# FFN weight sums in another order: A11 and A12 split as one tile, S3 and S2 made first, and the last product of a pair ahead of the next pair's S4

## The chip, the cores and the metric

The kernel runs on one core of one Trainium2 chip. The time is device microseconds of one execution. The kernel before takes 1554.56 us in the median of 3 runs (1554.34 to 1556.42).

## The reference

Two layers of a diffusion transformer work on 256 latent tokens and 256 context tokens, D = 1024, in float32. Layer 0 mixes the tokens by a short convolution, layer 1 by grouped-query attention. Around each mixer stand two gated FFNs, each of them modulated by shift, scale and gate of a conditioning vector:

```
def _swiglu(h, w13, w2):
    gte, up = jnp.split(h @ w13, 2, axis=-1)
    return (jax.nn.silu(gte) * up) @ w2
...
lat = lat + 0.5 * mod[:, 0, 2] * _swiglu(_modulate(lat, norm_g[i, 0], mod[:, 0, 0], mod[:, 0, 1]), ffn_w13[i, 0], ffn_w2[i, 0])
```

w13 is 1024 x 5632 and w2 is 2816 x 1024. In three of the four FFNs, (layer, block) = (0,0), (0,1) and (1,0), latent and context tokens go through the same weights, so that the kernel works on 512 columns of tokens; in the last, (1,1), only the 256 latent tokens are left. The change bears on the w13 product of the first three.

## The kernel before, in words

**Layout and precision.** Activations are held transposed, features on the 128 partitions and tokens along the free axis. Each float32 product is made of three matmuls on two parts of each operand (`mm3`, L133): hi x hi, hi x lo, lo x hi. The weights are split on the chip (`split`, L107): ScalarE (ACT) copies the raw tile to hi (L108), VectorE (DVE) subtracts hi from raw to make lo (L109). Raw tiles have eight buffers (`wr`, 1024 wide), hi and lo four each (`wh`, `wl`, 1024 wide, from `half`). `split_far` (L113 to L115) makes a lo without DVE: ACT writes hi and then -hi, and a DMA of GpSimd's queue adds the weight from memory onto it. Its tiles `w4h` and `w4l` have two buffers each.

**An FFN.** The hidden features come in 22 tiles of 128, cut into thirds of 8, 7 and 7 tiles (`THIRDS`). A third makes w13 for its tiles and then w2 (`project`, L581). In each FFN some first tiles are made in the plain way (six in (0,0), two in (0,1) and (1,0), by `w13_mm`, their results named pg and pu); all the others, 56 in the whole kernel, are *pairs*.

**A pair** (class `Pair`, L689 to L773) computes gate and up of one hidden tile by seven products in place of eight, in Winograd's form of Strassen's scheme. The weights of the tile are four blocks of 512 columns (up and gate, times the two halves of the features), A11, A12, A21 and A22, the activations four blocks of 256 tokens (B, with their sums T1 to T4). One product (`prod`) has four k-tiles of three matmuls, 128 x 256, into the banks p and q. The weight sums are S1 = A21 - A22 (as it is used here), S2 = A11 - S1, S3 = A22 - S2 and S4 = A12 - S2.

In `__init__` SyncE (SP) loads r2 (A22 and A12, 512 KB) and the right half of r1 (A11, 256 KB). GpSimd (POOL) writes the negation of r2's left half to r1's left half (L702), and a DMA of its queue adds A21 on it (L705): this is S1. A11 and A12 are split as two 512-wide pieces (L708 to L710). `sums(0)` makes S2 in r1's right half (L724), and `keep` splits r1 as S1 and S2. `sums(1)` copies A22 (`split_far` from r2's left half), subtracts S2 from both halves of r2 (L732) and splits r2 as S3 and S4.

**Order of the products.** `head` makes A11 and A12 (ACT copies p at L749), `five` S1 (copy L755), `six` S2 (copy L759) and S4, after which DVE adds q to the copy (L761) and ACT applies silu (L762); `seven` makes S3 and adds (L766), `four` makes A22, then gate times up (L772) and the split of the result into `gh` and `gl`. The loop in `ffn` delays `seven` and `four` into the next pair: A11, A12, S1, S3 of the previous pair, S2, S4, A22 of the previous pair. The last pair's `seven` and `four` are put between the first tiles of w2. After each pair `tick(0.9, at)` issues about one unit of modulation (DVE, L178), behind the previous pair's L766. The order on each engine and the semaphores come from a scheduling framework that follows the program's order and its dependences.

Of the kernel before, what the change touches and what calls it, by code (L numbers as in the profile page):

```python
# [16 lines left out]
P = 128  # L17
# [3 lines left out]
T2 = 2 * S  # L21
NM = 22
THIRDS = (8, 7, 7)

AS_IS = {(0, 0): range(3, 6), (0, 1): (), (1, 0): ()}

# [21 lines left out]
def hybrid_kernel(ctx: ExitStack, tc: tile.TileContext, a: dict, out: bass.AP):  # L48
# [640 lines left out]
    class Pair:  # L689
# [6 lines left out]
        def __init__(self, src, h):  # L696
            self.h, self.w, self.src = h, {}, src
            r2 = load_raw(src[:, 1024:2048])
            r1 = wp.tile([P, 1024], F32, name=nm("wr"), tag="wr", bufs=8)
            nc.sync.dma_start(r1[:, T2:], src[:, T2:1024])  # L700

            nc.gpsimd.tensor_scalar(  # L702
                out=r1[:, :T2], in0=r2[:, :T2], scalar1=-1.0, scalar2=None, op0=ALU.mult
            )
            nc.gpsimd.dma_start(out=r1[:, :T2], in_=src[:, :T2], accum_op=ALU.add)  # L705
            self.raw = [r1, r2]
            ts = half()
            for i, key in enumerate(("A11", "A12")):  # L708
                self.w[key] = [t[:, i * T2 : i * T2 + T2] for t in ts]
                split(*self.w[key], self.raw[i][:, T2:])  # L710

        def keep(self, keys, part):
            hi, lo = half()
# [4 lines left out]
        def sums(self, n):  # L718

            r1, r2 = self.raw  # L720
            s1, s2 = r1[:, :T2], r1[:, T2:]
            tt = nc.vector.tensor_tensor
            if n == 0:
                tt(out=s2, in0=s2, in1=s1, op=ALU.subtract)  # L724
                self.keep(("S1", "S2"), r1)
                return
            self.w["A22"] = [
                wp.tile([P, T2], F32R, name=nm(t), tag=t, bufs=2) for t in ("w4h", "w4l")
            ]
            split_far(*self.w["A22"], r2[:, :T2], self.src[:, 1024 : 1024 + T2])  # L730
            v = lambda t: t.rearrange("p (a c) -> p a c", a=2)
            tt(  # L732
                out=v(r2), in0=v(r2), in1=s2.unsqueeze(1).to_broadcast([P, 2, T2]),
                op=ALU.subtract,
            )
            self.keep(("S3", "S4"), r2)

        def prod(self, ps, wk, hk, first=True):
            for k in range(4):
# [14 lines left out]
            self.gm = tp.tile([P, T2], F32, name=nm("gm"), tag="gm", bufs=3)  # L754
            nc.scalar.copy(self.gm[:, S:], self.q1)  # L755

        def six(self):
            self.prod(self.p, "S2", "T2", False)
            nc.scalar.copy(self.sg[:, S:], self.p)  # L759
            self.prod(self.q1, "S4", ("B", 1, 1), False)  # L760
            nc.vector.tensor_tensor(out=self.sg, in0=self.q, in1=self.sg, op=ALU.add)  # L761
            nc.scalar.activation(out=self.sg, in_=self.sg, func=AF.Silu)  # L762
# [12 lines left out]
    def ffn(l, b, h, tot, gate, tail, gs=(), ev=(0, 0), z=None):  # L775
        gs = list(gs)
        i0 = 0
        for t, n in enumerate(THIRDS):
            between = ()
            if tot == T2:  # L780
                heads = []
                if t == 0 and not gs:

                    w = [load_w(a["w13"][l, b, 0])]
                    gs = [new_pair("g") for _ in range(2)]
                    pp = [(psum("pg"), psum("pu")) for _ in range(2)]
                    w13_mm(pp[0], w[0], h, range(KT), 0, S)
                    flush(1)
                    w.append(load_w(a["w13"][l, b, 1]))
                    at = w13_mm(pp[1], w[1], h, range(2), 0, S)  # L790
                    with tc.issue_after(at):
                        flush()
                    with tc.issue_after(every[-1]):
                        w13_mm(pp[1], w[1], h, range(2, KT), 0, S)
                    h.sums(0)
                    w13_mm(pp[0], w[0], h, range(KT), S, T2)
                    w13_post(pp[0], gs[0], 0, T2)
                    heads.append(Pair(a["w13"][l, b, 2], h))
                    h.sums(1)
                    heads[0].sums(0)  # L800
                    w13_mm(pp[1], w[1], h, range(KT), S, T2)
                    w13_post(pp[1], gs[1], 0, T2)
                    heads[0].head()
                    heads[0].sums(1)
                    h.sums(2)
                prev = None
                for i in range(len(gs), n):
                    if t == 0 and not heads and i in AS_IS[l, b]:
                        w = load_w(a["w13"][l, b, i])
                        pp = psum("pg"), psum("pu")  # L810
                        if prev:
                            prev.seven()
                        if "T1" not in h.t:
                            with tc.issue_after(rows["W1"]):
                                h.sums()
                        w13_mm(pp, w, h, range(4), 0, T2)
                        if prev:
                            gs.append(new_pair("g"))
                            prev.four(gs[-1])
                            prev = None  # L820
                        w13_mm(pp, w, h, range(4, KT), 0, T2)
                        gs.append(new_pair("g"))
                        tick(3, w13_post(pp, gs[-1], 0, T2))
                        continue
                    if heads:
                        pr = heads.pop(0)
                    else:
                        pr = Pair(a["w13"][l, b, i0 + i], h)
                        pr.sums(0)
                        pr.sums(1)  # L830
                        pr.head()
                    pr.five()
                    at = prev.seven().ins if prev else None
                    pr.six()
                    if prev:
                        gs.append(new_pair("g"))
                        prev.four(gs[-1])
                    prev = pr
                    if i:
                        tick(0.9, at)  # L840

                def last():
                    gs.append(new_pair("g"))
                    prev.four(gs[-1])

                between = (prev.seven, last) if prev else ()
            else:
                for i in range(n):
                    w = load_w(a["w13"][l, b, i0 + i])
                    gs.append(beside(gp.tile([P, T2], F32R, name=nm("gx"), tag="gh")))  # L850
                    pp = psum("pg"), psum("pu")
                    if i0 + i < EARLY:
                        for k in range(KT):
                            for j in range(2):
                                ps = pp[j][:, : z.w]
                                mm3(ps, w(at13(1 - j, k)), z.at(k), k == 0, k == KT - 1)
                            if i == 0 and k == KT // 2:
                                flush(1)
                        if i < 3:
                            flush(1)  # L860
                        early_post(pp, gs[i], z.ri)
                        tick(1)
                        continue
                    for j in range(2):
                        ws = [w(at13(1 - j, k)) for k in range(KT)]
                        mm_wide(pp[j], ws, [h.both(k) for k in range(KT)], True, True)
                    beside_post(pp, gs[i])
                    tick(1)
            i0 += n

            def ws2(m):
                src = a["w2a"][l, b, m // 2] if t == 0 else a["w2b"][l, b, t - 1, m // 2]
                o = (m % 2) * n * P
                raw = load_raw(src[:, o : o + n * P], n * P)
                hi, lo = half()
                split(hi[:, : n * P], lo[:, : n * P], raw[:, : n * P])
                return lambda k: (hi[:, k * P : k * P + P], lo[:, k * P : k * P + P])

            cur = gs
            end = t == len(THIRDS) - 1  # L880
            project(
                ws2,
                (lambda k, c0, c1: cur[k]) if tot == S
                else lambda k, c0, c1: (cur[k][0][:, c0:c1], cur[k][1][:, c0:c1]), n,
                gate, tail if end else None, tot, 2 if end and tot == T2 else 0, ev[end], between,
            )
            gs = []
# [527 lines left out]
def _layout(inp):  # L1415
# [17 lines left out]
    d["modb"] = f("mod_b").reshape(2, 72, P).transpose(2, 0, 1)  # L1433
    d["normg"] = f("norm_g").reshape(2, 3, KT, P).transpose(3, 0, 1, 2)
    w13 = f("ffn_w13").reshape(2, 2, 2, KT // 2, P, 2, NM, P)[:, :, :, :, :, ::-1]
    d["w13"] = w13.transpose(0, 1, 6, 4, 2, 5, 3, 7).reshape(2, 2, NM, P, 2048)
    w2 = f("ffn_w2").reshape(2, 2, NM, P, KT // 2, 2, P)
    w2 = w2.transpose(0, 1, 4, 3, 5, 2, 6)
    n0, n1 = THIRDS[:2]
# [53 lines left out]
```

## Time and profile before

| | before |
|---|---|
| median of 3 runs | 1554.56 us |
| profiled execution | 1554.59 us |
| its span | 1552.8 us |
| TensorE (PE) busy | 1544.5 us, 99% |
| VectorE (DVE) busy | 1283.3 us, 83% |
| ScalarE (ACT) busy | 783.6 us, 50% |
| GpSimd (POOL) busy | 221.1 us, 14% |
| DMA, read from memory | 259.45 MB, 168 GB/s over the span |

Times in the rows are microseconds from the start of the span. A group of instructions has its line, engine and operation, output and input tiles, shapes and count, then the busy time, the mean of one in ns, and the idle time ahead of them with what ended it. A row of the timeline has start, duration, engine, line and operation; "x3" joins neighbours of one kind. A matmul's duration includes its time in the pipeline, so the pace is read from the starts.

### The profile page before, as it was taken

To read this page: it belongs to the slowest core of one execution; us is meant where nothing else is said; L and a number is where in the kernel's file an instruction comes from. 1 tells how busy PE (TensorE), PEld (TensorE's weight loads), DVE (VectorE), ACT (ScalarE), POOL (GpSimd) and SP (SyncE) were. 2 spreads that over 40 slices of the span, in tenths; PEclk is the share of its full clock that TensorE was granted. 3 is DMA by queue.
4 is the path that set the end of the run, shared out by engine and by line. 5 is a ranking of instruction groups with operands and counts; after the bars stand their busy time and mean duration, and the time that the engine had idled before them with its cause. 6 is when DMAs were issued, how large, how long until landed. Compare 5 with 4: busy or idle time off the path is not lost.

```text
span 1552.8 us, 26276 instructions
## 1 busy us (share of the span) xinstructions
PE 1544.5 (99%) x10252; PEld 1416.9 (91%) x10252; DVE 1283.3 (83%) x2003; ACT 783.6 (50%) x1297; POOL 221.1 (14%) x187
## 2 busy tenths in 40 slices
PE   9999999999999999999999999999999999999999
PEld 7898998998888899989999899989999899998888
DVE  5788789799987489968978889968978878888676
ACT  5642553644422366436446476436346456774553
POOL 0012212200000012033042012022041002300000
PEclk9999999999999999999999999999999999999999
DMA  9567467475565325655656635655766753376552
GB/s 373 195 181 198 105 191 195 120 193 170 182 200 180 115 62 132 207 137 141 205 144 161 199 75 136 199 154 127 227 177 176 258 163 116 95 237 220 170 195 75
DMA packets 88254, 263.53 MB, mean 170 GB/s; under 512 B 10817, under 2 KB 12609, under 8 KB 88129
## 3 DMA queue, kind: packets, MB, share of 16 engines
q1 hardware_dynamic: 69408, 230.72, 45.8%
q0 software_dynamic: 16128, 29.37, 11.3%
q10 hardware_dynamic: 2592, 1.76, 0.4%
q8 instruction: 80, 1.31, 0.4%
q14 instruction: 46, 0.37, 0.1%
HBM read 259.45 MB, written 1.05 MB: 168 GB/s over the span
## 4 chain that ended last, share of the span: by engine, by line
PE 97%; DVE 1%; ACT 1%; issue 0%; POOL 0%; DVEq 0%; ACTq 0%; POOLq 0%
PE py L138 9%; PE py L137 9%; PE py L139 9%; PE p L139 7%; PE p L138 7%; PE p L137 7%; PE q L139 5%; PE q L137 5%; PE q L138 5%; PE py L145 2%; PE pu L145 2%; PE pg L145 2%; PE py L147 1%; PE pg L147 1%; PE pu L147 1%; PE pv L137 1%
## 5 line engine op out<-in xcount | busy, mean ns | idle before, releaser
L108 ACT ACTIVATE wh<-wr 128x1024 fp32r<-128x1024 f32 (+2 forms) x446 | 395.5, 914 | 332.3 <-PE py L138 127.7
L109 DVE TENSOR_TENSOR wl<-wr,wh 128x1024 fp32r<-128x1024 f32 (+2 forms) x446 | 457.2, 1049 | 84.2 <-ACT wh L108 65.0
L178 DVE CUSTOM_DVE_ANT_0 junk<-wr,scbc,modb 128x1024 bf16<-128x1024 f32 x213 | 274.6, 1289 | 9.1 <-DMA wr<-in_modT 7.4
L138 PE MATMUL py<-gl,wh 128*128 128x512 f32 (+1 forms) x570 | 213.4, 374 | 0.0
L137 PE MATMUL py<-gh,wh 128*128 128x512 f32 (+1 forms) x570 | 213.3, 374 | 0.0
L139 PE MATMUL py<-gh,wl 128*128 128x512 f32 (+1 forms) x570 | 212.9, 373 | 0.0
L702 POOL TENSOR_SCALAR wr<-wr 128x512 f32<-128x512 f32 x56 | 100.8, 1800 | 535.2 <-DMA wr<-in_w 306.2
L564 DVE SCALAR_TENSOR_TENSOR x<-py,mod,x 128x256 f32<-128x256 f32 x213 | 94.3, 478 | 66.9 <-PE py L139 55.4
L138 PE MATMUL p<-tl,wh 128*128 128x256 f32 x448 | 126.8, 283 | 0.0
L139 PE MATMUL p<-th,wl 128*128 128x256 f32 x448 | 126.8, 283 | 0.0
L137 PE MATMUL p<-th,wh 128*128 128x256 f32 x448 | 126.7, 283 | 0.0
L139 PEld LDWEIGHTS py<-gh,wl 128*128 128x128 f32 x570 | 107.3, 188 | 19.1
L137 PEld LDWEIGHTS py<-gh,wh 128*128 128x128 f32 x570 | 107.4, 188 | 18.4
L138 PEld LDWEIGHTS py<-gl,wh 128*128 128x128 f32 x570 | 107.4, 188 | 18.0
L115 POOL DMA_DIRECT2D w4l<-in_w x56 | 54.2, 968 | 449.4 <-ACT w4l L114 415.4
L138 PE MATMUL q<-bl,wh 128*128 128x256 f32 x320 | 90.6, 283 | 0.0
L139 PE MATMUL q<-bh,wl 128*128 128x256 f32 x320 | 90.6, 283 | 0.0
L137 PE MATMUL q<-bh,wh 128*128 128x256 f32 x320 | 90.6, 283 | 0.0
L137 PEld LDWEIGHTS p<-th,wh 128*128 128x128 f32 x448 | 86.0, 192 | 0.4
L138 PEld LDWEIGHTS p<-tl,wh 128*128 128x128 f32 x448 | 86.0, 192 | 0.3
L139 PEld LDWEIGHTS p<-th,wl 128*128 128x128 f32 x448 | 86.0, 192 | 0.0
L762 ACT ACTIVATE sg<-sg 128x512 f32<-128x512 f32 x56 | 35.4, 632 | 90.4 <-DVE sg L761 90.4
(303 smaller groups left out, 4061.2 us busy)
## 6 DMA issues: line engine op xcount, KB each, us to landing
wr<-in_w SPq DMA_DIRECT2D x120, 512.0 KB, 4.8
wr<-in_modT SPq DMA_DIRECT2D x117, 512.0 KB, 5.0
wr<-in_w2b SPq DMA_DIRECT2D x64, 448.0 KB, 4.0
wr<-in_w2a SPq DMA_DIRECT2D x32, 512.0 KB, 4.5
wr<-in_w SPq DMA_DIRECT2D x56, 256.0 KB, 3.7
wr<-in_w POOLq DMA_DIRECT2D x56, 256.0 KB, 5.8
w4l<-in_w POOLq DMA_DIRECT2D x56, 256.0 KB, 5.9
pm<-in_mod SPq DMA_DIRECT2D x16, 512.0 KB, 10.2
```

Source lines behind the costliest of these rows:

```text
L108: nc.scalar.activation(out=hi, in_=src, func=AF.Copy)
L109: return nc.vector.tensor_tensor(out=lo, in0=src, in1=hi.bitcast(F32), op=ALU.subtract)
L115: nc.gpsimd.dma_start(out=lo, in_=src, accum_op=ALU.add)
L137: nc.tensor.matmul(ps, wh, mh, start=first, stop=False, **kw)
L138: nc.tensor.matmul(ps, wh, ml, start=False, stop=False, **kw)
L139: return nc.tensor.matmul(ps, wl, mh, start=False, stop=last, **kw).ins
L145: nc.tensor.matmul(ps, w[0], m[2], start=first and n == 0, stop=False)
L147: nc.tensor.matmul(ps[:, :S], w[1], m[0], start=False, stop=last and n == len(ms) - 1)
L178: nc.vector.tensor_tensor_reduce(out=junk, in0=raw, in1=scbc[:, v, :], scale=0.5 if ch in (2, 8) else 1.0, scalar=modb[:, l, col : col + 1 ...
L564: ins = nc.vector.scalar_tensor_tensor(out=x[:, m, s * S : s * S + S], in0=ps[:, o : o + S], scalar=g[:, m, s : s + 1], in1=x[:, m, s * S ...
L702: nc.gpsimd.tensor_scalar(out=r1[:, :T2], in0=r2[:, :T2], scalar1=-1.0, scalar2=None, op0=ALU.mult)
L762: nc.scalar.activation(out=self.sg, in_=self.sg, func=AF.Silu)
```

## The change

The order of the blocks in memory is changed for the tiles that pairs work on: quarters 1 and 2 are exchanged. So r2 holds A11 and A12 side by side and is split at once; r1's right half holds A22, and its left half becomes A21 - A11, which is S3. `sums(0)` now copies A22, makes S2 = A22 - S3 in its place and splits r1 as S3 and S2; `sums(1)` subtracts S2 from both halves of r2 and splits r2 as S1 = A11 - S2 and S4 = A12 - S2. `two` (S2) is cut out of `six` (S4). The loop's order becomes A11, A12, S3 of the previous pair, S2, S1, A22 of the previous pair, S4; in the first pair of a third, A11, A12, S1, S2, S4.

```diff
+SINGLE = {(0, 0): 6, (0, 1): 2, (1, 0): 2}
...
             nc.gpsimd.dma_start(out=r1[:, :T2], in_=src[:, :T2], accum_op=ALU.add)
             self.raw = [r1, r2]
-            ts = half()
-            for i, key in enumerate(("A11", "A12")):
-                self.w[key] = [t[:, i * T2 : i * T2 + T2] for t in ts]
-                split(*self.w[key], self.raw[i][:, T2:])
+            self.keep(("A11", "A12"), r2)
...
             r1, r2 = self.raw
-            s1, s2 = r1[:, :T2], r1[:, T2:]
+            s2 = r1[:, T2:]
             tt = nc.vector.tensor_tensor
             if n == 0:
-                tt(out=s2, in0=s2, in1=s1, op=ALU.subtract)
-                self.keep(("S1", "S2"), r1)
+                self.w["A22"] = [
+                    wp.tile([P, T2], F32R, name=nm(t), tag=t, bufs=2) for t in ("w4h", "w4l")
+                ]
+                split_far(*self.w["A22"], s2, self.src[:, T2:1024])
+                tt(out=s2, in0=s2, in1=r1[:, :T2], op=ALU.subtract)
+                self.keep(("S3", "S2"), r1)
                 return
-            self.w["A22"] = [
-                wp.tile([P, T2], F32R, name=nm(t), tag=t, bufs=2) for t in ("w4h", "w4l")
-            ]
-            split_far(*self.w["A22"], r2[:, :T2], self.src[:, 1024 : 1024 + T2])
             v = lambda t: t.rearrange("p (a c) -> p a c", a=2)
             tt(
                 out=v(r2), in0=v(r2), in1=s2.unsqueeze(1).to_broadcast([P, 2, T2]),
                 op=ALU.subtract,
             )
-            self.keep(("S3", "S4"), r2)
+            self.keep(("S1", "S4"), r2)
...
-        def six(self):
+        def two(self):
             self.prod(self.p, "S2", "T2", False)
             nc.scalar.copy(self.sg[:, S:], self.p)
+
+        def six(self):
             self.prod(self.q1, "S4", ("B", 1, 1), False)
...
-                    pr.five()
-                    at = prev.seven().ins if prev else None
-                    pr.six()
                     if prev:
+                        at = prev.seven().ins
+                        pr.two()
+                        pr.five()
                         gs.append(new_pair("g"))
                         prev.four(gs[-1])
+                    else:
+                        at = None
+                        pr.five()
+                        pr.two()
+                    pr.six()
                     prev = pr
...
+    for (l, b), n in SINGLE.items():
+        w13[l, b, n:] = w13[l, b, n:, :, (0, 2, 1, 3)].transpose(1, 2, 0, 3)
+    d["w13"] = w13.reshape(2, 2, NM, P, 2048)
```

More of the change, by code (lines that the diff above doesn't have):

```diff
@@ L1435, in _layout @@
     w13 = f("ffn_w13").reshape(2, 2, 2, KT // 2, P, 2, NM, P)[:, :, :, :, :, ::-1]
-    d["w13"] = w13.transpose(0, 1, 6, 4, 2, 5, 3, 7).reshape(2, 2, NM, P, 2048)
+    w13 = w13.transpose(0, 1, 6, 4, 2, 5, 3, 7).reshape(2, 2, NM, P, 4, 512).copy()
+    for (l, b), n in SINGLE.items():
+        w13[l, b, n:] = w13[l, b, n:, :, (0, 2, 1, 3)].transpose(1, 2, 0, 3)
+    d["w13"] = w13.reshape(2, 2, NM, P, 2048)
     w2 = f("ffn_w2").reshape(2, 2, NM, P, KT // 2, 2, P)
```

## The prediction

> **What bounds the kernel now.** I read the page first: its head, the row of granted clock, and the chain that ended last.
>
> ```profile
> span 1552.8 us, 26276 instructions
> ...
> PE 1544.5 (99%) x10252; PEld 1416.9 (91%) x10252; DVE 1283.3 (83%) x2003; ACT 783.6 (50%) x1297; POOL 221.1 (14%) x187
> ...
> PEclk9999999999999999999999999999999999999999
> ...
> PE 97%; DVE 1%; ACT 1%; issue 0%; POOL 0%; DVEq 0%; ACTq 0%; POOLq 0%
> ```
>
> TensorE is busy for 1544.5 of 1552.8 us at full clock, and 97% of the chain runs on it. VectorE is busy for 83%, which is high but not the bound. A share is an average, though, so the stage that the change touches has to be looked at by itself. The next view lists the waits of TensorE (waiter, releaser: sum, times, longest), and the one after it gives two stretches in which pairs run one after the other (length, then busy times of PE, PEld, DVE, ACT and POOL, clock, DMA share, GB/s).
>
> ```profile
> PE pv L137 <- ACT hh L310: 1.4, 1, 1.4
> PE idle L897 <- DVE eps_t L88: 1.0, 1, 1.0
> PE pg L138 <- DVE bl L109: 0.8, 2, 0.4
> PE pg L1000 <- ACT hh L973: 0.7, 2, 0.4
> PE pu L1000 <- DVE wl L109: 0.5, 1, 0.5
> ```
>
> ```profile
> 592.40:643.00 50.60, 50.60 (x416) 50.27 (x415) 46.11 (x61) 32.93 (x54) 9.20 (x9) 1.00 0.66 172
> 697.00:747.00 50.00, 50.00 (x419) 50.00 (x418) 42.30 (x58) 31.11 (x55) 11.98 (x10) 1.00 0.60 148
> ```
>
> No product of a pair (their tiles are p and q) is among the largest waits; those stand at the start, in the mixer and in the FFN's first tiles (pg, pu). In both stretches of pairs TensorE is busy for the whole stretch, 50.60 of 50.60 and 50.00 of 50.00 us. VectorE has 46.11 of 50.60 us there, 91%, which is near full. The matmuls show how tight the row is, and the one place of a stretch of pairs where I found it broken:
>
> ```profile
> 590.65 0.28 PE L137 MATMUL q<-bh,wh 128*128 128x256 f32 x1
> 590.96 0.38 PE L139 MATMUL p<-bh,wl 128*128 128x256 f32 x1
> ```
>
> ```profile
> 714.75 0.28 PE L138 MATMUL p<-tl,w4h 128*128 128x256 f32 x1
> 714.87 0.28 PE L139 MATMUL p<-th,w4l 128*128 128x256 f32 x1
> 714.99 0.28 PE L137 MATMUL p<-bh,wh 128*128 128x256 f32 x1
> ```
>
> A matmul starts every 0.12 us (714.75, 714.87, 714.99), also across the border of one pair's last product (w4h, w4l) and the next pair's first. A product is 12 of them, 1.44 us, and a pair seven products, 10.08 us. At the first pairs of the second FFN one start is 0.31 us behind the last (590.65, 590.96), 0.19 us late.
>
> **The ceiling of a gain.** The change removes no matmul: the build has the same 9576 rows on TensorE, in another order. So it can save only what TensorE waits for inside the pairs. That is nothing in the two stretches, and 0.2 us at the start of the second FFN; I count the third FFN's start, which has the same code, as 0.2 as well: 0.4 us in all. The 1.4, 1.0, 0.8, 0.7 and 0.5 us waits above belong to code that the change leaves alone.
>
> **What goes.** A11 and A12 were split as two 512-wide pieces, and are one 1024-wide now. The groups by shape, DVE and then ACT:
>
> ```profile
> L109 DVE TENSOR_TENSOR wl<-wr,wh 128x1024 fp32r<-128x1024 f32 x250 | 304.2, 1225 | 66.4 <-ACT wh L108 52.9 <-ACT sg L669 9.5 <-PE pu L147 3.1
> L109 DVE TENSOR_TENSOR wl<-wr,wh 128x512 fp32r<-128x512 f32 x132 | 87.0, 696 | 12.4 <-ACT wh L108 12.1
> ```
>
> ```profile
> L108 ACT ACTIVATE wh<-wr 128x1024 fp32r<-128x1024 f32 x250 | 263.5, 1060 | 234.1 <-PE py L138 72.5 <-DVE wr L724 56.9 <-PE p L138 27.4
> L108 ACT ACTIVATE wh<-wr 128x512 fp32r<-128x512 f32 x132 | 76.1, 621 | 31.2 <-PE py L138 24.2 <-PE q L138 2.5 <-PE pu L138 2.4
> ```
>
> Per pair DVE saves 2 x 0.696 - 1.225 = 0.167 us and ACT 2 x 0.621 - 1.060 = 0.182 us; over 56 pairs, 9.4 and 10.2 us. All of it lies beside the products, since TensorE has no idle time there, so I cost it at nothing. DMAs are as many and as large as before (per pair SP's two loads, POOL's negation at L702 and the two adding DMAs at L705 and L115); their contents are permuted on the host, ahead of the launch. A22 is now read from the early right half of r1, so POOL's queue is not lengthened.
>
> **What moves: the slack.** This is where the change can hurt, so I laid one pair's steps out against the products. Before, DVE and ACT around one end of A22 (columns: start, duration):
>
> ```profile
> 711.03 0.43 DVE L766 TENSOR_TENSOR p<-p,gm 128x256 f32<-128x256 f32 x1
> 711.36 1.28 DVE L178 CUSTOM_DVE_ANT_0 junk<-wr,scbc,modb 128x1024 bf16<-128x1024 f32 x1
> ...
> 712.56 1.22 DVE L109 TENSOR_TENSOR wl<-wr,wh 128x1024 fp32r<-128x1024 f32 x1
> 713.82 0.69 DVE L761 TENSOR_TENSOR sg<-q,sg 128x512 f32<-128x512 f32 x1
> 715.19 0.69 DVE L772 TENSOR_TENSOR gm<-sg,p 128x512 f32<-128x512 f32 x1 [0.68 <-PE p L139]
> 715.80 1.23 DVE L732 TENSOR_TENSOR wr<-wr,wr 128x1024 f32<-128x1024 f32 x1
> 716.95 0.69 DVE L109 TENSOR_TENSOR gl<-gm,gh 128x512 fp32r<-128x512 f32 x1
> 718.16 2.44 DVE L109 TENSOR_TENSOR wl<-wr,wh 128x1024 fp32r<-128x1024 f32 x3 [0.53 <-ACT wh L108]
> 720.52 0.68 DVE L724 TENSOR_TENSOR wr<-wr 128x512 f32<-128x512 f32 x1
> ```
>
> ```profile
> 715.08 0.62 ACT L113 ACTIVATE w4h<-wr 128x512 fp32r<-128x512 f32 x1
> 715.73 0.63 ACT L114 ACTIVATE w4l<-w4h 128x512 fp32r<-128x512 f32 x1
> 716.27 0.62 ACT L108 ACTIVATE gh<-gm 128x512 fp32r<-128x512 f32 x1
> ```
>
> The last matmul of A22 gives way to the next pair at 714.99, and DVE's L772 starts 0.20 us later (715.19). The 512-wide steps follow each other every 0.61 us (715.19, 715.80) and the 1024-wide ones every 1.15 (715.80, 716.95); L766 takes 0.33 and a modulation unit 1.20 (711.03, 711.36, 712.56). The split of S3 and S4 (the first of the three at 718.16) ends by 718.16 + 1.22 = 719.38; S4, the sixth product, needs its lo part from its third matmul on, at 714.99 + 5 x 1.44 + 0.24 = 722.43. Its slack is 3.0 us.
>
> After, the order of the products is A11, A12, S3 of the previous pair, S2, S1, A22 of the previous pair, S4. Let X be the end of A22; S4 runs to X+1.44, A11 to 2.88, A12 to 4.32, S3 to 5.76, S2 to 7.20, S1 to 8.64, A22 to 10.08. Read from the build, DVE's order per pair is: product gate times up (L772), second sum s2 (L724), first sums (L732), lo of g, L761, lo of S3|S2, lo of S1|S4, L766, a modulation unit, lo of A11|A12. With the spacings above:
> - L772 at X+0.20; s2 at +0.81 (ACT's copy w4h, 715.08 against 714.99, starts at +0.09 and is done at +0.71, ahead of it); done at +1.49.
> - L732 now needs that s2, 0.10 us more for the dependence (my estimate, no row of before has it; 0 to 0.2): +1.59 to +2.82.
> - lo of g +2.73, L761 +3.33, lo of S3|S2 +3.93 to +5.15. S2's third matmul is at X + 5.76 + 0.24 = 6.00. With 0.06 for the hand-over (590.96 against the end of 589.80 + 1.10, below) the slack is **0.79 us**.
> - lo of S1|S4 +5.07 to +6.29, needed at 7.20 + 0.24 = 7.44: slack 1.1 us. L766 +6.2, needed at 8.64: 2 us. The modulation unit +6.5, lo of A +7.74 to +8.96, needed by the next A11 at 11.76: 2.7 us.
>
> ```profile
> 589.80 1.10 DVE L109 TENSOR_TENSOR wl<-wr,wh 128x512 fp32r<-128x512 f32 x1
> ```
>
> ACT's hi parts come earlier: w4h, w4l, hi of g, then hi of S3|S2 at about +1.8 to +2.9, before DVE asks. DVE's load per pair is 0.06 us less (the merged split saves 2 x 0.60 - 1.14 in spacing), some 8.5 of 10.08 us. So in the steady row TensorE is not stopped, but the nearest deadline moves from 3.0 to 0.79 us. If the cover goes, the cost is what exceeds 0.79, per pair, over the 38 steady pairs of the build (of 56; the others stand next to a third's start or end).
>
> **The first pair of a third** has no previous pair: A11, A12, S1, S2, S4. There S1 waits for both sums now instead of one: s2 0.68, L732 1.23, hi 1.06, lo 1.22, of which the sums' wait is at most L732 and a split later than before, 1.23 + 1.22 = 2.45 us. Inside the FFN these stand beside 21 or more matmuls of w2 and A11 and A12 (2.88 us), so I cost them at nothing. At the start of the second and third FFN the lo of S1|S4 comes some 0.3 us ahead of its use by my layout, while the lo of the second pair's A, late by 0.19 us in before, comes earlier. I take the gain of 0.4 and keep 0 to 1.8 us loss for the range (a whole split of 1.22 late less 0.3, twice).
>
> The sum, against the profiled execution of 1554.59 us (1552.8 of span and 1.8 around it): 0 for splits, 0 for sums and order, -0.4 at the two starts, **1554.2 us**. The median of the runs shown, 1554.56, is that execution's time to 0.03.
>
> **A row that speaks against it.** POOL's negation of 512 columns stands once in every pair, and can meet a split on DVE:
>
> ```profile
> L702 POOL TENSOR_SCALAR wr<-wr 128x512 f32<-128x512 f32 x56 | 100.8, 1800 | 535.2 <-DMA wr<-in_w 306.2
> ```
>
> ```profile
> 667.95 2.29 POOL L702 TENSOR_SCALAR wr<-wr 128x512 f32<-128x512 f32 x1 [0.16 <-DMA wr<-in_w]
> ```
>
> ```profile
> 668.81 1.62 DVE L109 TENSOR_TENSOR wl<-wr,wh 128x1024 fp32r<-128x1024 f32 x1
> ```
>
> Here a split took 1.62 instead of 1.22 us while the negation took 2.29 instead of 1.80. [...]
>
> **Rivals.**
> 1. **Slower: the chain from the end of A22 to the lo of S3|S2 overruns.** Three DVE steps on it have two SBUF inputs and could meet POOL (L732, lo of g, lo of S3|S2). If each gains 0.4 us, as at 668.81, it is 1.2 - 0.79 = 0.41 us late in each of 38 pairs: 15.6 us, 1570. It decides from 0.79 us on. For it: DVE at 91% and the shortened slack. Against it: one negation of 1.8 us can't cover three steps that span 3.6 us, and the mean of 250 splits, 1.225, shows that meetings are rare. Chance 0.09.
> 2. **Slower: the first pairs stall.** If the lo of S1|S4 is late by one more split of ACT (1.06 us) at nine first pairs, 9.5 us, 1564. For it: S1 waits for both sums; against it: the w2 products before it. Chance 0.07. Only at the two FFN starts, 1.8 us, 1556.4: chance 0.12.
> 3. **Faster: the saved instructions were on the path.** 9.4 us of DVE, 1545. For it only the 91%; against it TensorE's 50.60 of 50.60 us. Chance 0.03. [...]
> 4. **The change doesn't do what it says.** The build shows the new order and 55 or 56 rows fewer on DVE and ACT, so 0.01, with before's time.
>
> **How the numbers follow.** The forecast has the remaining 0.68. 0.2%, 3.1 us, is about what a measurement of this kernel can tell from no change. Within it lie the forecast, the stall at two starts, and no effect: 0.68 + 0.12 + 0.01 = 0.81. Slower by more: 0.09 + 0.07 = 0.16. Faster: 0.03. The range runs from 1553.2 (the forecast, and 1 us more for waits that I couldn't find in the list) to 1558.0 (the stall of 1.8 us doubled to four places); beyond it lie 0.19.
>
> **What would show it.** Right: TensorE busy for all of a stretch of pairs, A22 of the previous pair followed by S4 at a spacing of 0.12; DVE's lo of S3|S2 ending about 5.2 us after the end of A22; splits x56 fewer on 512 columns. Wrong: waits of p or q on wl in the list, once a pair (rival 1) or at first pairs (rival 2). A span shorter than 1550 us would say that TensorE's spacing hides waits that I read as its pace.

## The result and the profile after

The changed kernel takes 1562.99 us in the median of 4 runs (1561.83 to 1563.11), the kernel before 1554.66; the ratio is 1.0051, with a 95% interval of 1.0039 to 1.0062. The ratios here and below are taken over the fast runs, as all the runs here are, and are not quotients of the medians shown. The change makes the kernel 8.3 us slower, where 1554.2 was forecast and 1558.0 was the range's upper end. The profiled execution took 1563.11 us, with a span of 1561.2. From the page after:

```profile
span 1561.2 us, 26137 instructions
...
PE 1546.1 (99%) x10252; PEld 1418.2 (91%) x10252; DVE 1275.9 (82%) x1947; ACT 776.6 (50%) x1241; POOL 228.3 (15%) x187
...
PE 94%; DVE 2%; DMA 2%; ACT 1%; POOL 1%; issue 0%; DVEq 0%; POOLq 0%; ACTq 0%
```

DVE and ACT are busy 7.4 and 7.0 us less, where the merged split was to save 9.4 and 10.2, and it did not help. The chain that ended last has 94% on PE in place of 97%, and DMA, absent before, has 2%. The waits of PE after (two rows of the view) name a place that was not among those of before:

```profile
PE ss L272 <- DVE acc L265: 6.0, 3, 4.6
...
PE q L141 <- DVE wl L111: 0.8, 1, 0.8
```

`ss` is the small matmul that adds up the squares for a norm; it waits for VectorE's running sum `acc`. This has nothing to do with pairs. To see where the 8.4 us arose, I laid the start of the n-th matmul of the one trace beside that of the other; both have 10252:

| stretch (us in before) | after minus before |
|---|---|
| start, up to 13 | -0.7 |
| a norm near 375 | +0.15 |
| conv mixer's end, 550 to 566 | +7.3 (7.4 up to 557, 0.1 of it made up) |
| first pairs of the second FFN, 590 to 597 | -0.36 |
| end of the second FFN, near 902 | +0.9 |
| first pairs of the third FFN, 937 to 950 | -0.36 |
| third third of the third FFN, 1147 to 1153 | +1.4, and +0.2 up to 1231 |
| last FFN, 1391 | -0.2 |
| all other stretches, the steady pairs among them | 0.0 |

The chain after, around the first of them (start, duration, step):

```profile
548.32 5.43 DMA wr<-in_w
553.95 0.69 DVE wr L727
554.64 0.41 DVE x L566
555.07 0.42 ACT sq L263
555.52 0.43 DVE acc L265
555.95 0.41 DVE x L566
556.37 0.42 ACT sq L263
556.82 0.43 DVE acc L265
557.30 1.01 PE ss L272 x4
```

L727 is s2, the second weight sum of a pair of the *next* FFN. Behind it in VectorE's rows stand the mixer's last residual updates (L566) and the sums of squares (L265); none of those starts ahead of s2's row at 553.95. VectorE's rows say how long it stood, after first and then before:

```profile
548.18 0.68 DVE L265 TENSOR_TENSOR acc<-acc,sq 128x512 f32<-128x512 f32 x1
553.95 0.69 DVE L727 TENSOR_TENSOR wr<-wr 128x512 f32<-128x512 f32 x1 [5.09 <-DMA wr<-in_w]
```

```profile
548.12 0.69 DVE L263 TENSOR_TENSOR acc<-acc,sq 128x512 f32<-128x512 f32 x1
548.83 0.48 DVE L564 SCALAR_TENSOR_TENSOR x<-py,mod,x 128x256 f32<-128x256 f32 x1
...
592.02 0.68 DVE L724 TENSOR_TENSOR wr<-wr 128x512 f32<-128x512 f32 x1
```

In VectorE's rows from 545.1 to 548.2 the two executions agree to 0.1 us. Then the changed kernel's VectorE waits 5.09 us for the second pair's transfer, which the kernel before reads at 592.02, 38 us later. The transfer is not issued later; POOL's rows before and after:

```profile
546.38 1.49 POOL L702 TENSOR_SCALAR wr<-wr 128x512 f32<-128x512 f32 x1 [1.54 <-DVE wl L109]
548.27 0.90 POOL L705 DMA_DIRECT2D wr<-in_w  x1 [0.41 <-POOL wr L702]
```

```profile
546.44 1.48 POOL L704 TENSOR_SCALAR wr<-wr 128x512 f32<-128x512 f32 x1 [6.85 <-DVE wl L111]
548.32 0.91 POOL L707 DMA_DIRECT2D wr<-in_w  x1 [0.41 <-PE py L141]
```

It was issued at 548.27 and at 548.32. Only what waits for it differs.

**Why s2 stands there.** Counted in the traces, s2 of the first two pairs of the second FFN is VectorE's row 742 and 757 before, and row 674 and 683 after, ahead of the residual updates. Of these 68 and 74 rows, some 16 to 18 are splits that were merged in the pairs up to there; by the other 50 and more s2 has moved ahead. The code says what may have let them move. Before, s2 overwrites A11, so it waits for DVE's own split of A11, which in turn waits for a buffer of wh and wl. After, s2 overwrites A22, whose only other reader is ACT's copy to w4h, for which a buffer is free. So after, s2 is ready as soon as its transfer is. That the framework orders instructions by when it takes them to be ready, and counted on a shorter transfer here than the 5.43 us of the chain, is an inference from the place and is not shown. The place itself is read from the traces, and the experiments e3 and e4 below show that it comes with the new blocks and sums. VectorE's waits for these transfers in the whole span, before and after:

```profile
DVE wr L724 <- DMA wr<-in_w: 6.1, 3, 4.5
```

```profile
DVE wr L727 <- DMA wr<-in_w: 31.7, 12, 5.1
```

All twelve waits after stand at the first two pairs of a third; in the steady pairs s2 waits for no transfer. The wait has a second price. PE's rows around it, before and then after:

```profile
552.95 0.28 PE L137 MATMUL py<-zh,wh 128*128 128x256 f32 x1
553.22 0.60 PE L270 MATMUL ss<-ones,acc 128*128 128x1 f32 x4
```

```profile
552.40 0.28 PE L139 MATMUL py<-zh,wh 128*128 128x256 f32 x1
...
563.23 0.41 PE L141 MATMUL py<-zh,wl 128*128 128x256 f32 x1
563.44 0.41 PE L139 MATMUL py<-zh,wh 128*128 128x256 f32 x1
563.65 0.34 PE L140 MATMUL py<-zl,wh 128*128 128x256 f32 x1
563.83 0.28 PE L141 MATMUL py<-zh,wl 128*128 128x256 f32 x1
563.94 0.28 PE L139 MATMUL py<-zh,wh 128*128 128x256 f32 x1
```

From 552.40 to 557.30 no matmul starts (557.30 is the first row of ss in the chain above), where before the same two starts are 0.27 us apart (552.95, 553.22): 4.6 us. Then the matmuls of 256 columns start every 0.21 us, until from 563.83 on they start every 0.12 again. Laid beside before, the 30 matmuls from 557.30 up to there lose another 2.8 us. The sum, 7.4, is the step up to 557 in the table. The granted clock of this stretch is half (columns as in the prediction's view of stretches; the clock is the 0.50):

```profile
557.00:563.70 6.70, 6.40 (x30) 6.40 (x31) 3.63 (x11) 2.97 (x8) 0.00 (x0) 0.50 0.00 0
```

At 1154 us of the changed kernel (1147 to 1153 in the table) an early s2 costs time in another form; VectorE's rows after:

```profile
1146.92 0.69 DVE L727 TENSOR_TENSOR wr<-wr 128x512 f32<-128x512 f32 x1 [4.56 <-DMA wr<-in_w]
1150.04 0.69 DVE L727 TENSOR_TENSOR wr<-wr 128x512 f32<-128x512 f32 x1 [2.43 <-DMA wr<-in_w]
...
1152.57 1.22 DVE L731 TENSOR_TENSOR wr<-wr,wr 128x1024 f32<-128x1024 f32 x1
```

The second pair's s2 waits until 1150.04 ahead of the first pair's broadcast subtraction (L731), so that S1's lo is late: these are the 0.8 us of q on wl.

### The profile page after: what moved, and what is told of

It reads as the page before. It is cut to its first block, busy times and chain, and to the rows that moved or that the text cites. A ratio compares the mean times of both kernels' runs of the same rounds, so it can differ in the third digit from the quotient of the medians.

```text
span 1561.2 us, 26137 instructions
## 1 busy us (share of the span) xinstructions
PE 1546.1 (99%) x10252; PEld 1418.2 (91%) x10252; DVE 1275.9 (82%) x1947; ACT 776.6 (50%) x1241; POOL 228.3 (15%) x187
## 4 chain that ended last, share of the span: by engine, by line
PE 94%; DVE 2%; DMA 2%; ACT 1%; POOL 1%; issue 0%; DVEq 0%; POOLq 0%; ACTq 0%
PE py L140 8%; PE py L139 8%; PE py L141 8%; PE p L139 7%; PE p L141 7%; PE p L140 7%; PE q L141 5%; PE q L140 5%; PE q L139 5%; PE py L147 2%; PE pu L147 2%; PE pg L147 2%; DMA wr<-in_w 2%; PE py L149 1%; PE pg L149 1%; PE pu L149 1%
## 5 line engine op out<-in xcount | busy, mean ns | idle before, releaser
L111 DVE TENSOR_TENSOR wl<-wr,wh 128x1024 fp32r<-128x1024 f32 (+2 forms) x390 | 452.6, 1176 | 61.7 <-ACT wh L110 42.2
L704 POOL TENSOR_SCALAR wr<-wr 128x512 f32<-128x512 f32 x56 | 107.1, 1913 | 750.6 <-DVE wl L111 367.0
L566 DVE SCALAR_TENSOR_TENSOR x<-py,mod,x 128x256 f32<-128x256 f32 x213 | 94.2, 478 | 42.1 <-PE py L141 30.5
L773 DVE TENSOR_TENSOR gm<-sg,p 128x512 f32<-128x512 f32 x56 | 38.5, 687 | 54.9 <-PE p L141 54.9
## 6 DMA issues: line engine op xcount, KB each, us to landing
pm<-in_mod SPq DMA_DIRECT2D x16, 512.0 KB, 10.2
```

The source lines that it names most:

```text
L111: return nc.vector.tensor_tensor(out=lo, in0=src, in1=hi.bitcast(F32), op=ALU.subtract)
L566: ins = nc.vector.scalar_tensor_tensor(out=x[:, m, s * S : s * S + S], in0=ps[:, o : o + S], scalar=g[:, m, s : s + 1], in1=x[:, m, s * S ...
L704: nc.gpsimd.tensor_scalar(out=r1[:, :T2], in0=r2[:, :T2], scalar1=-1.0, scalar2=None, op0=ALU.mult)
L773: nc.vector.tensor_tensor(out=self.gm, in0=self.sg, in1=self.u, op=ALU.mult)
```

## The experiments

Theory A is the one above: an s2 that waits for its transfer holds up VectorE's other work. Its rivals: the transfers are late by themselves (B); the slack of the steady pairs is used up (C); the order of the products costs the time (C'). The first 26 us of the profiled executions come out 0.7 us shorter (the changed kernel) to 2.2 us longer (e1, e4) than before's, though the change bears on nothing there; the mean granted clock of the profiled execution is 0.999 in e1 and e4, where before has 1.000. So besides the medians I give the place in the trace, in the time of before.

**e1: s2 of the first two pairs tied behind later work, at two FFNs.**

```diff
+                self.first = tt(out=b11, in0=b12, in1=b11, op=ALU.subtract).ins
...
-                tt(out=s2, in0=s2, in1=r1[:, :T2], op=ALU.subtract)
+                with tc.issue_after(behind) if behind else nullcontext():
+                    tt(out=s2, in0=s2, in1=r1[:, :T2], op=ALU.subtract)
...
-                    heads[0].sums(0)
+                    heads[0].sums(0, h.first)
...
-                        pr.sums(0)
+                        pr.sums(0, prev.far if prev and i == 3 and (l, b) != (0, 0) and t == 0 else None)
```

`h.first` is the first activation sum, `prev.far` the previous pair's broadcast subtraction.

> The changed kernel, with the second sum (s2) of the first two pairs of the second and third FFN tied behind later VectorE work: the first pair's behind the first activation sum (T1), the second pair's behind the first pair's broadcast subtraction. Nothing else is changed. Theory A (in the changed kernel these two s2 stand early in VectorE's order, ahead of the residual update and the sum of squares, and wait there for POOL's adding DMA): the 4.6 us wait of ss at 557 us, the slow matmuls after it and the 0.85 us wait at 909 us go, about 8.0 us, so 1555.0 us. Theory B (the pairs' transfers are late by themselves, and the wait only moves to the pairs' own products): at most 2 us are saved, 1561 to 1563. Theory C (the loss comes from the shortened slack in the steady pairs): no change, 1563.

Measured: 1556.32 us in the median of 11 runs, against 1554.72 of before beside it; ratio 1.0005 (0.9997 to 1.0014). The 7.3 us near 557 are gone. In its profiled execution 2.2 of the 2.5 us to before arose in the first 26 us; 0.4 are left near 902 and 0.5 near 1148. B and C fall.

**e2: every s2 behind the previous pair's broadcast subtraction.** The condition of e1's last line is only `if prev`.

> As e1, and every other pair's s2 is tied behind the previous pair's broadcast subtraction too, which moves only the second pair of the later thirds. Theory A: also the 1.4 us at the first pair near 1155 us go, where two s2 that wait for DMAs stand ahead of the first pair's broadcast subtraction: 1553.6 us, so 0.5 to 1 us under the kernel before (the two first pairs of FFNs start 0.3 us earlier there). Theory B: 1561 to 1563. Theory C: 1563.

Measured: 1554.57 us (11 runs); ratio 0.9998 (0.9990 to 1.0007). No q or p of a pair is left among PE's waits, and the step near 1148 is gone. The half microsecond to 1 us under before did not come: 0.7 us are still lost near 902. ScalarE's rows of e2 show by what:

```profile
898.78 0.63 ACT L115 ACTIVATE w4h<-wr 128x512 fp32r<-128x512 f32 x1 [1.83 <-DMA wr<-in_w]
899.32 0.61 ACT L263 ACTIVATE sq<-x 128x512 f32<-128x512 f32 x1
```

The copy of A22 was moved ahead as well, on ScalarE, and a square for the norm stands behind it.

**e9: those copies tied too,** behind ScalarE's copies of the activation sums.

```diff
+                with tc.issue_after(act) if act else nullcontext():
+                    split_far(*self.w["A22"], s2, self.src[:, T2:1024])
```

> e2, and ScalarE's copies of A22 for the first two pairs of the second and third FFN tied behind ScalarE's copies of the activation sums (T1 for the first pair, T4 for the second). In e2 such a copy waits 1.8 us for its transfer near 898 us, ahead of a square for the norm, and ss still waits 0.7 us for the sum of squares. Theory A (an instruction that waits for a transfer holds up what stands behind it on its engine, whichever engine it is): the 0.7 us go, 1553.9 us, 0.7 under the kernel before. Theory B (that wait has another cause): 1554.6 us, as e2.

Measured: 1556.25 us (11 runs); ratio 1.0011 (1.0002 to 1.0020). This was a miss. Near 902 nothing is lost any more, as theory A has it. The wait of ss fell from 1.1 us in two places to 0.5 in one, and another came in its place. From PE's waits of e9:

```profile
PE p L139 <- ACT sg L762: 0.9, 2, 0.5
```

Tied so late, the copies stand among the first pairs' own work on ScalarE, and products now wait there: 0.7 us are lost near 586 and 0.6 near 937. No version was found that beats the kernel before.

**e10 and e11: which of the two.** e1's ties for the second pair alone, and for the first pair alone.

> The changed kernel with only the second pair's s2 tied (the one that waits 5.1 us for its transfer at 548.9 to 553.9 us). Theory A: nearly all of the loss near 557 us goes, as in e1: 1555.0 to 1556.3 us.

> The changed kernel with only the first pair's s2 tied (the one that waits 3.8 us for its transfer, up to 541.0 us). Theory A: the second pair's s2 still stands ahead of the residual update and the sum of squares, and the loss stays: 1562 to 1563 us. If the first s2 were the cause: 1555 to 1556 us.

Measured: e10 1555.04 us (10 runs; ratio 1.0004, 0.9995 to 1.0013), as expected. e11 1558.70 us (1557.21 to 1562.43, 5 runs; ratio 1.0031, 1.0019 to 1.0043), where 1562 to 1563 was expected: one of its five executions came out there. The rows of e11's profiled execution (1557.35 us), VectorE and then PE:

```profile
552.18 0.69 DVE L728 TENSOR_TENSOR wr<-wr 128x512 f32<-128x512 f32 x1 [3.66 <-DMA wr<-in_w]
```

```profile
555.53 0.61 PE L272 MATMUL ss<-ones,acc 128*128 128x1 f32 x4 [2.44 <-DVE acc L265]
...
556.20 0.28 PE L141 MATMUL py<-zh,wl 128*128 128x256 f32 x1
556.32 0.28 PE L139 MATMUL py<-zh,wh 128*128 128x256 f32 x1
```

The second s2 still waits, but it is released at 552.18 in place of 553.95: without the first s2 ahead of it, VectorE freed the second pair's buffer earlier, and POOL's negation ran at 545.29 in place of 546.44. PE's wait is 2.4 in place of 4.6 us, and after it the matmuls start every 0.12 us at once. So the second s2 holds PE up, and the first makes it later. Whether slow matmuls follow it is shown for this execution alone: the granted clock over the whole of it is 1.000, as in the other of 1557 us, but 0.997 to 0.998 in the three slower ones (1558.70 to 1562.43 us), near the 0.997 to 0.998 of the changed kernel. Those were not profiled.

**e5: idle matmuls during the wait.** Twenty matmuls on a tile of ones stand ahead of ss in the changed kernel, 18 of them right ahead of it; nothing else is changed. The trace has two rows for each.

> The changed kernel with 20 idle matmuls of 128 columns ahead of the ss matmuls near 557 us (18 of them directly ahead), so that TensorE works during the wait for the sum of squares. The wait itself stays. Theory A1 (of the 7.1 us lost there, 4.8 are the wait and 2.4 are matmuls that start every 0.21 instead of 0.12 us after it, because TensorE had been idle): the slow matmuls go, 1563.0 - 2.4 = 1560.6 us. Theory A2 (the slow matmuls wait for their data, which the late VectorE also delays): no change, 1563.

Measured: 1560.89 us (4 runs; ratio 1.0043, 1.0029 to 1.0057), 2.1 under the changed kernel. PE's rows of e5:

```profile
553.47 4.18 PE L275 MATMUL ss<-ones 128*128 128x128 f32 x36
558.95 0.60 PE L278 MATMUL ss<-ones,acc 128*128 128x1 f32 x4 [1.30 <-DVE acc L265]
...
560.78 0.28 PE L139 MATMUL py<-zh,wh 128*128 128x256 f32 x1
560.90 0.29 PE L140 MATMUL py<-zl,wh 128*128 128x256 f32 x1
```

The wait stays, and is longer: ss starts 5.3 us late against before, in place of 4.6. But the matmuls after it start every 0.12 us (560.78, 560.90), and the mean granted clock of this execution is 1.000, where the changed kernel's has 0.998. Theory A1 holds: the slow matmuls come of PE's idleness, not of late data.

**e4: the new order of the products alone,** with before's blocks and sums: `two` cut out of `six`, and the loop as in the change.

> The kernel before's blocks, splits and sums, with the products in the changed order (S3 of the previous pair, S2, S1, A22 of the previous pair, S4). Theory A: s2 stays late in VectorE's order, since it still overwrites A11 after its split; 1554.0 to 1555.5 us, as before. Theory C' (the order of the products costs the time): 1561 to 1563.

Measured: 1556.37 us (11 runs; ratio 1.0007, 0.9998 to 1.0016), 1.7 over before. In its profiled execution 2.2 of 3.0 us arose in the first 26 us and 0.8 in small steps among the pairs. s2 stays late in VectorE's order (581.50 and 594.77 us for the first two pairs of the second FFN), and nothing is lost near 557. C' falls.

**e3: the new blocks and sums alone,** with before's order of the products.

```diff
...
+                    pr.five()
+                    at = prev.seven().ins if prev else None
+                    pr.two()
+                    pr.six()
+                    if prev:
+                        gs.append(new_pair("g"))
+                        prev.four(gs[-1])
```

> The changed kernel's blocks and sums, with the products in the order of the kernel before (A11, A12, S1, S3 of the previous pair, S2, S4, A22 of the previous pair). Theory A: the early s2 stay where they are, so the 7 to 8 us stay; and S1, whose lo part comes 6.3 us after the end of A22, is wanted after 3.1 us, so that each of 38 steady pairs waits 2 to 3 us more: 1640 to 1690 us. Theory C' (the order of the products is what costs the time): 1555.

Measured: 1583.97 us (2 runs; ratio 1.0183, 1.0164 to 1.0201). The wait of ss is there (5.0 us), with 7.3 us at that place, and each steady pair loses 0.5 us, not 2 to 3: the size was wrong. Both halves of A hold in direction: with the new sums and the old order of the products the steady pairs lose time, which they don't in the changed kernel, and the early s2 comes with the blocks and sums.

**e6 and e7: the slack measured.** e2 with one or two more 512-wide steps on s2, in the 47 pairs that have a previous pair.

```diff
+                    if behind and behind is not getattr(self.h, "first", None):
+                        for _ in range(1):
+                            tt(out=s2, in0=s2, in1=s2, op=ALU.max)
```

> e2 (all s2 tied) with one more 512-wide VectorE step on s2 (the maximum of s2 with itself) behind s2, in each pair that has a previous pair, 47 in all. It lengthens the chain to the lo of S3|S2 by 0.79 us (0.69 and 0.10 for the dependence). The slack worked out in the prediction is 0.79 us, so theory A expects 0 to 0.05 us per steady pair, 1554.6 to 1557 us. Theory C (the slack in the changed kernel is already used up): 0.7 us or more in each of 38 pairs, 1581 and more.

> As e6, with two more steps, 1.58 us: by the slack of 0.79 us each of 38 steady pairs is 0.79 us late, 30 us, 1585 us. If the slack is larger than the layout says (over 1.6 us): 1555 us. If there was none: 60 us, 1615 us.

Measured: e6 1562.16 us (4 runs; ratio 1.0050, 1.0036 to 1.0063), e7 1581.11 us (4 runs; ratio 1.0171, 1.0157 to 1.0185). e6 lies above the 1554.6 to 1557 that was expected, e7 near its 1585. In the traces a steady pair loses 0.17 us in e6, where 0 to 0.05 was expected, and 0.59 in e7, where 0.79 was; the remainder stands mostly at the first pairs. From PE's waits of e7:

```profile
PE q L139 <- ACT wh L110: 13.2, 40, 0.3
```

If nothing else moved, one step of 0.79 us that costs 0.17 would leave a slack of 0.6 us, and two of 1.58 that cost 0.59 one of 1.0. But more moved. In e6 VectorE splits S3|S2 ahead of the broadcast subtraction, and it is the lo of S1 that comes late; in e7 the products of S2 and S1 are interleaved on PE, and q waits for S1's hi. So the layout's 0.79 us for the lo of S3|S2 was not measured by itself. What the two runs show is that one more step costs far less than its length, so that the pairs had some slack, and that two cost most of one. C, by which there is none, falls with e6 as it does with e2.

**e8: A11 and A12 as two halves again,** on e2.

> e2 with A11 and A12 split as two 512-wide pieces again instead of one of 1024. VectorE has 0.17 us more per pair and ScalarE 0.18, 9.4 and 10.2 us over 56 pairs. If these lie beside the products, as the prediction has it: 1554.6 us, as e2. If the merged split saves time on the path: up to 1564 us.

Measured: 1554.73 us (11 runs; ratio 1.0002, 0.9993 to 1.0011), 0.2 us from e2. The merged split is worth nothing that can be measured, as it was costed.

## Why the prediction was wrong

**The bound and the ceiling: right.** PE sets the pace, and the only gain that the change brought was at the starts of the second and third FFN: 0.36 us at each, where 0.2 was taken.

**What goes: right.** DVE's saving lay beside the products (e8). The splits of 512 columns took 0.696 us each before, the merged ones after 1.227 us in the mean, and the difference, 2 x 0.696 against 1.227 us a pair, moved no time of the kernel.

**The steady pairs: the layout was right, to 0.01 us.** The rows after, PE and DVE:

```profile
709.85 0.28 PE L139 MATMUL q<-bh,wh 128*128 128x256 f32 x1
...
715.85 0.28 PE L141 MATMUL p<-th,wl 128*128 128x256 f32 x1
```

```profile
710.05 0.69 DVE L773 TENSOR_TENSOR gm<-sg,p 128x512 f32<-128x512 f32 x1 [2.03 <-PE p L141]
710.66 0.69 DVE L727 TENSOR_TENSOR wr<-wr 128x512 f32<-128x512 f32 x1
711.45 1.23 DVE L731 TENSOR_TENSOR wr<-wr,wr 128x1024 f32<-128x1024 f32 x1
...
713.79 2.35 DVE L111 TENSOR_TENSOR wl<-wr,wh 128x1024 fp32r<-128x1024 f32 x2
```

With X = 709.85, L773 starts at X+0.20, s2 at +0.81, L731 at +1.60, the lo of S3|S2 at +3.94 and is wanted at +6.00: the layout had 0.20, 0.81, 1.59, 3.93 and 6.00. By these rows the slack fell to 0.8 us, and nothing overran it. Rival 1, the overrun by steps that meet POOL, did not come about: POOL's negation rose to 1.91 us in the mean, and in the steady pairs nobody waited for it. Steps did meet it. Before, each kind that the rival names was longer somewhere under a negation (L732 1.45 us at 1141.41, mean 1.23; a lo of g 1.10 at 307.99, mean 0.71; a split 1.63 at 1149.76, mean 1.23), and after, L731 took 1.44 us at 617.47, mean 1.24.

**The step that failed: "Inside the FFN these stand beside 21 or more matmuls of w2 and A11 and A12 (2.88 us), so I cost them at nothing."** The starts of the second and third FFN were costed in the same way, at a gain of 0.4 us and a loss of at most 1.8, and the sum has "0 for sums and order". The first pairs were costed by when their results are wanted. That says how late an instruction may come; it does not say how early it is placed. The order on VectorE was read from the build for the steady pairs only. At the conv mixer's end s2 stands more than 50 rows further ahead among its neighbours, and the question that belonged there (what is queued behind an instruction that waits) was asked for the steady chain and not for that place. It cost 7.3 us with the matmuls that it slowed. The first two s2 cost 1.4 us in the third third of the third FFN as well, and with ScalarE's copies of A22, which came early in the same way (e2, e9), 0.9 at the end of the second FFN.

**The rivals.** Rival 2 named first pairs, with 9.5 us, near the 8.3 measured, which is luck: its mechanism, lo parts of S1|S4 that are late by a split of ACT, explains 1.4 us at one of nine places at most, and there it was the second pair's s2 that made it late. The larger part was no stall of a pair.

**The chances.** 0.16 for slower was too little: they covered stalls of the products alone, and none for a wait in work that the diff doesn't name.

## What to carry to other kernels

Where a scheduler orders the instructions, a change that removes a dependence can also remove what held an instruction back: look in the built order for each instruction that became ready earlier, and at what now stands behind it on its engine, in the neighbouring stages too. An instruction that waits for a transfer should be placed by the transfer's latest landing, or be tied behind the work that it would block, but no later than its own readers allow (e9). A wait of TensorE is to be counted with the slow matmuls that may follow it (2.8 us behind one of 4.6 us here).

## What the runs showed of the hardware

- **The clock after a wait.** After a wait of 4.6 us without a matmul, 128x256 matmuls started every 0.213 us up to 563.8 us, in place of 0.120, and the granted clock was 0.50 from 557.0 to 563.7. After 2.4 us without one none was slow in e11's profiled execution. With TensorE kept busy for most of the wait (e5: matmuls for 4.18 us, then 1.30 us without one) none was slow either.
- **An operation that reads its predecessor's output on VectorE** started 0.79 us after it in 35 of the 43 places where L731 stands right behind s2 in the trace after (s2 at 710.66, L731 at 711.45), where independent ones of that width start 0.61 apart (710.05, 710.66): the prediction's estimate of 0.10 for the dependence, on top of the 0.69, is what the row shows. The trace of before has it too, where the prediction found no row: s2 at 689.83, L732 at 690.62.
